# A hybrid two-block layer on Trainium2: a ninth weight tile, the last two pairs' down products last, and three pieces of work moved

## The chip, the cores and the metric

One core of a Trainium2 chip runs the whole program. The metric is the device time of one execution in microseconds (us), median of several. TensorE multiplies (PE in the rows; PEld its weight loads), VectorE (DVE), ScalarE (ACT) and GpSimd (POOL) do the rest, SyncE (SP) issues nearly all DMAs. Data are held in SBUF, 128 partitions; matrix products end in PSUM, eight banks of 128 x 512 float32.

## The reference

Two blocks work on 512 tokens of width 1024 in float32. The first is a mixer (state space and windowed attention) and a mixture of 64 experts, the second a mixer (neighbourhood attention, "na", and gated linear attention) and an MLP. What the change touches:

```python
# first block: 512 tokens, 8 groups of 8 experts, the two best of one group
expert_id = g_sel[:, None] * EXPERTS_PER_GROUP + top_local
gate = jax.nn.softmax(top_logit, axis=-1) * p_group
...
hid = jax.nn.silu(xb @ w_gate[e]) * (xb @ w_up[e])     # 1024 x 512 each
return hid @ w_down[e]                                 # 512 x 1024
...
y = jnp.zeros_like(t).at[tok_sorted].add(y_buf[dest] * flat_g[order][:, None])
# between the blocks
x = rmsnorm(h, norm_final)
# second block
n = rmsnorm_2(h, ln_g)
proj = n @ w_in                                        # q, k, v of na, and the gated part
```

## The kernel before

A planner orders the instructions of each engine from the text of the kernel; `pin` keeps an instruction in program order on its engine, and `order(a, b)` puts b behind a.

**Weights.** Each expert has three matrices of 2 MiB, 384 MiB in all. They come through a ring of eight SBUF tiles of 16 KB a partition: three of `ringp`, two of `ring2`, the two that hold A1 and A2 in the first block (`w16x`), and one of `ring3`, which is opened in `moe` where the mixer's pools lay. `ring` (line 119) takes the next tile, `load` (149) cuts the load into pieces, and SyncE's queue issues them in the order gate, up, down of each pair. A piece is issued as soon as its part of the tile has been read. For the last pair `pair` (137) loads the two experts' tiles in turn, piece by piece.

**Pairs.** `experts` goes over 32 pairs of experts, 64 slots for each expert, so that a pair's 128 rows fill the partitions. For pair i: gate and up products of the rows `xg` into two banks `pj` (line 991; 32 records a product), silu and product to `hid`, four transposes, `hT`, then the down products in two halves (`y`, `tp`), each split into a rounded part and its rest (`yH`, `yL`). A 0/1 matrix `ST` (made by `way` from the tokens of the slots) brings the rows back to H: `combine` makes two products (yH, yL) for each of 4 token tiles and 2 halves and adds the bank to H (line 1157, and the sum at 1160). The sums of pair i - 1 are made in pair i by `bring`.

**Rows.** The tokens of the slots are found by `values` for two pairs at a time (`slots`, L828), fetched from DRAM by GpSimd's indirect DMA (`fetch`, L843) into four tiles `rows`, and turned by `gained` into `xg` (two buffers, L1018) one pair ahead. Slots that nobody has are left out of the fetch, so the rows are zeroed once before (line 984).

**Ahead of pair 0.** The router's last choices run on VectorE (`choose`, `gather_first`: `eq` at 939, `S` at 940). The rows of pair 0 are made by products with H (L943), then turned. `split_values` (815 to 817) prepares on GpSimd what `values` needs; the zeroing (984) and the counting tile `tt` (988) stand ahead of it in GpSimd's order.

**The last pair.** It does not wait for H to be complete. `Begin` (the start of the second block) turns H, with all pairs up to 30 in it, into eight PSUM banks (`turn`, line 1704, four transposes a bank), the last pair's rows are added to the banks by two products each (`mm(p, y, ST)`), and `split` rounds them to `n2H`, `n2L`. Then `combine` brings the last pair to H, and `norms` loads the second block's first weights `wv` (line 1720) and makes the factors `r`. Eight of pair 30's sums stand inside the last gate product:

```python
if last and p is pg and j in (2, 5):
    bring(4)
```

**The second block's start.** `neighbours` makes four value projections (L199, L178 to 180), sends `r` to DRAM and reads it back in another order as `rc` (lines 1362 and 1365), and only then turns the values into seven tiles `v` scaled by `rc` (1376 to 1381), ahead of the projections of q and k (`project`). `attend` comes one head pair later than `project`. Each product of three terms is made from a rounded part and its rest, split by ScalarE (158) and VectorE (159).

Of the kernel before, what the change touches and what calls it, by code (L numbers as in the profile page):

```python
# [28 lines left out]
class Net:  # L29
# [83 lines left out]
    def ring(self, shape, dma, parts=1):  # L113
# [698 lines left out]
    def split_values(self):  # L812
# [4 lines left out]
        Pl.tensor_tensor(self.parts10[:, :, :, 1], v, self.parts10[:, :, :, 0].bitcast(FT), OP.subtract)  # L817
# [145 lines left out]
    def experts(self, keep, pool, front, inner, then):  # L963
        nc, i = self.nc, self.ins
        mm = nc.tensor.matmul
# [6 lines left out]
        def weights(e0):  # L972
            n = 4 if e0 < 12 else 4 if e0 == 62 else 2
            if e0 == 62:
                return [self.pair(shape, (w[62], w[63])) for shape, w in (([P, KT, 512], wg), ([P, KT, 512], wu),
                                                                          ([P, 4, D], wd))]
            return ([self.ring([P, KT, 512], wg[e0 + s], 8 if e0 == 2 else n) for s in range(2)],
                    [self.ring([P, KT, 512], wu[e0 + s], n) for s in range(2)],
                    [self.ring([P, 4, D], wd[e0 + s], n) for s in range(2)])
        ahead = None  # L980
# [7 lines left out]
        nc.gpsimd.iota(tt, pattern=[[1, T]], base=-1023, channel_multiplier=0, allow_small_or_imprecise_dtypes=True)  # L988
# [51 lines left out]
        self.split_values()  # L1040
# [3 lines left out]
        def bring(n):  # L1044
            for _ in range(min(n, len(todo))):
                self.combine(*todo.pop(0), pin=True)

        for i in range(32):
# [3 lines left out]
            G, U, Dn = ahead or weights(e0)  # L1052
            ahead = None
            pg, pu = self.psum("pj"), self.psum("pj")
            X = Xs.pop(i)
            for W, p in ((G, pg), (U, pu)):
                for j in range(KT):
# [3 lines left out]
                    if last and p is pg and j in (2, 5):  # L1061
                        bring(4)
                if i == 0 and p is pg:
                    values(0)
            if i == 0:
                chosen(1)
            if last:
# [19 lines left out]
            hT = pool.tile([P, 4, P], FT, name="hT", bufs=1)  # L1087
# [9 lines left out]
            def down(y, s, j, hs):  # L1097
                mm(y[64 * s:64 * s + 64, :], hT[:, j, 64 * s:64 * s + 64], Dn[s][:, j, hs], start=j == 0, stop=j == 3)
            if not last:
                for half, hs in enumerate(halves):  # L1100
# [7 lines left out]
                    todo.extend((ST, yH, yL, t, hs) for t in range(NT))  # L1108
                if i == 0:
                    values(1)  # L1110
                    for _ in gained(1):
                        evicted()
            else:
                ys = [self.psum(t) for t in ("y", "pj")]
# [4 lines left out]
                if begin:  # L1119
                    turned += [begin.turn(k) for k in (4, 5)]  # L1120
                parts = []
                for y in ys:
                    yH = pool.tile([P, 512], FR, name="yH")
                    yL = pool.tile([P, 512], FR, name="yL")
                    self.split(yH, yL, y, g)
                    parts.append((yH, yL))
                if begin:
                    turned.append(begin.turn(6))
                    for k in range(KT):
                        p = turned[k]  # L1130
                        for x, y in enumerate(parts[k // 4]):
                            mm(p, y[:, k % 4 * P:k % 4 * P + P], ST, start=False, stop=x == 1)
                        begin.split(k, p)
                        if k == 0:
                            turned.append(begin.turn(7))
# [17 lines left out]
    def combine(self, ST, yH, yL, t, hs, n=P, pin=False):  # L1153
        nc, h = self.nc, self.H
        p = self.psum("sc")
        for k, y in enumerate((yH, yL)):
            m = nc.tensor.matmul(p, ST[:n, t * P:(t + 1) * P], y[:n], start=k == 0, stop=k == 1)  # L1157
# [16 lines left out]
    def overflow(self, keep, pool, front):  # L1174
# [5 lines left out]
        orow = front.tile([64, D], FT, name="orow", tag="xg", bufs=2)  # L1180
        nc.gpsimd.memset(orow, 0.0)
# [3 lines left out]
        with tc.If(self.count > 0):  # L1185
            with tc.For_i(0, self.count, 1):
# [50 lines left out]
                for half in range(2):  # L1237
# [7 lines left out]
                    for t in range(NT):  # L1245
                        self.combine(ST, yH, yL, t, hs, 64)
# [95 lines left out]
    def neighbours(self, small, pool, wp, mixp, w_in, A):  # L1342
# [29 lines left out]
        v = []  # L1372
        for n in range(7):
            p = self.psum("tp")
            for j in range(4):
# [419 lines left out]
```

## Time and profile before

| | |
|---|---|
| three runs | 2061.43, 2054.8 and 2062.07 us |
| the profiled execution | 2057.0 us, span 2055.2 us |
| mean granted TensorE clock | 0.982 of full speed |
| TensorE busy | 1943.0 us, 95% |
| VectorE, ScalarE, GpSimd busy | 955.6, 533.8 and 196.3 us |
| bytes moved by DMA | 494.25 MB |

The first block's mixer takes the first 380 us or so, the router and the start of the experts lie around 380 to 440, the experts go on to about 1372, and the second block follows. Times in rows count from the first instruction of the span. A timeline row has start, length, engine, line, operation, out<-in, form and count; a row with a count merges neighbours of one kind, and its length runs to the end of the last. A granted clock of 1.00 is 2.4 GHz and 0.50 is 1.2 GHz.

### The profile page before, as it was taken

How to read it: one execution, taken by the hardware profiler on the slowest of the kernel's cores; microseconds unless marked ns; L12 is line 12 of the kernel's file. 1: busy time of each engine (PE TensorE's matmuls, PEld its weight loads, DVE VectorE, ACT ScalarE, POOL GpSimd, SP SyncE). 2: the span in 40 equal slices, each digit the busy share in tenths (PEclk: the TensorE clock that was granted, in tenths of full speed). 3: DMA queues.
4: the chain of work that ended last, by engine and by line, in shares of the span. 5: the costliest groups of instructions: out<-in, count | busy, mean ns of one | idle time of the engine just before them, and what ended most of it. 6: DMA issues, size and time to landing. Idle time of an engine off the chain costs nothing.

```text
span 2055.2 us, 24059 instructions
## 1 busy us (share of the span) xinstructions
PE 1943.0 (95%) x9519; PEld 1228.8 (60%) x9519; DVE 955.6 (46%) x1896; ACT 533.8 (26%) x899; POOL 196.3 (10%) x248
## 2 busy tenths in 40 slices
PE   7999999989999999989999999998999999999998
PEld 6788777734444444434434434446777778888886
DVE  5764667733543234244324323334564764343345
ACT  5773535311100000000000000024342433232232
POOL 5211324110000000000000000003201110000000
PEclk9999999999999999999999999999999999999999
DMA  7312122779999999999999999973212112213211
GB/s 201 113 42 82 46 78 82 287 299 416 415 423 425 424 424 424 424 424 424 425 425 424 421 421 425 423 252 67 90 42 82 42 42 92 94 71 123 90 74 41
DMA packets 114778, 494.25 MB, mean 240 GB/s; under 512 B 16492, under 2 KB 23091, under 8 KB 74984
## 3 DMA queue, kind: packets, MB, share of 16 engines
q1 hardware_dynamic: 107720, 483.63, 58.8%
q0 software_dynamic: 6352, 6.96, 1.5%
q10 hardware_dynamic: 592, 2.10, 0.3%
q8 instruction: 76, 1.25, 0.2%
q14 instruction: 38, 0.31, 0.0%
HBM read 500.68 MB, written 6.15 MB: 247 GB/s over the span
## 4 chain that ended last, share of the span: by engine, by line
PE 46%; DMA 44%; DVE 5%; ACT 3%; issue 1%; POOL 0%; SPq 0%; DVEq 0%; ACTq 0%; POOLq 0%
DMA w<-in_w_down 14%; DMA w<-in_w_up 14%; DMA w<-in_w_gate 13%; PE pj L179 7%; PE pj L178 7%; PE pj L180 7%; PE sc L179 3%; PE sc L178 3%; PE sc L180 3%; PE pj L991 2%; DMA w<-in_w_in 1%; DVE M L697 1%; PE y L180 1%; PE y L178 1%; PE y L179 1%
## 5 line engine op out<-in xcount | busy, mean ns | idle before, releaser
L991 PE MATMUL pj<-w,xg 128*64 128x512 f32 x1536 | 369.1, 612 | 39.4 <-DMA w<-in_w_up 36.4
L991 PEld LDWEIGHTS pj<-w,xg 128*64 128x64 f32 x1536 | 126.8, 141 | 270.8 <-issue 202.1
L159 DVE TENSOR_TENSOR wL<-w,wH 128x1024 fp32r<-128x1024 f32 x135 | 167.3, 1240 | 202.3 <-ACT wH L158 201.7
L1079 DVE SCALAR_TENSOR_TENSOR hid<-pj,slots,hid 128x512 f32<-128x512 f32 x32 | 24.1, 752 | 458.2 <-PE pj L991 458.2
L158 ACT CAST wH<-w 128x1024 fp32r<-128x1024 f32 x136 | 142.3, 1047 | 339.8 <-PE pj L179 165.9
L1160 DVE TENSOR_TENSOR H<-sc,H 128x512 f32<-128x512 f32 x256 | 161.5, 683 | 10.8 <-PE sc L1157 8.3
L991 PE MATMUL pj<-w16x,xg 128*64 128x512 f32 x512 | 125.1, 602 | 10.5 <-DMA w16x<-in_w_up 10.5
L1157 PE MATMUL sc<-yH,ST 128*128 128x512 f32 x256 | 113.2, 442 | 0.6 <-DVE H L1160 0.6
L1088 ACT COPY hT<-tp 128x512 f32<-128x512 f32 x32 | 18.8, 586 | 346.4 <-PE tp L1086 346.4
L843 POOL DMA_INDIRECT rows<-hd,tok x31 | 31.1, 1002 | 802.8 <-issue 642.0
L180 PE MATMUL pj<-n3H,wL 128*128 128x512 f32 (+1 forms) x272 | 103.6, 381 | 0.8 <-DVE wL L159 0.8
L178 PE MATMUL pj<-n3H,wH 128*128 128x512 f32 (+1 forms) x272 | 103.6, 381 | 0.0
L179 PE MATMUL pj<-n3L,wH 128*128 128x512 f32 (+1 forms) x272 | 103.5, 380 | 0.0
L178 PE MATMUL pj<-A,wH 128*128 128x512 f32 x240 | 97.8, 407 | 4.0 <-ACT wH L158 2.8
L1157 PE MATMUL sc<-yL,ST 128*128 128x512 f32 x256 | 101.2, 395 | 0.0
L179 PE MATMUL sc<-wL,mixH 128*128 128x512 f32 x252 | 98.5, 391 | 0.0
L178 PE MATMUL sc<-wH,mixH 128*128 128x512 f32 x252 | 98.4, 391 | 0.0
L180 PE MATMUL sc<-wH,mixL 128*128 128x512 f32 x252 | 98.2, 390 | 0.0
L179 PE MATMUL pj<-A,wH 128*128 128x512 f32 x240 | 97.6, 407 | 0.0
L180 PE MATMUL pj<-A,wL 128*128 128x512 f32 x240 | 96.8, 403 | 0.5 <-DVE wL L159 0.5
L991 PEld LDWEIGHTS pj<-w16x,xg 128*64 128x64 f32 x512 | 47.8, 138 | 82.2 <-issue 60.1
L991 PE MATMUL y<-w,hT 128*64 128x512 f32 x384 | 91.8, 599 | 0.7 <-ACT hT L1088 0.7
(571 smaller groups left out, 3322.2 us busy)
## 6 DMA issues: line engine op xcount, KB each, us to landing
w<-in_w_down SPq DMA_DIRECT2D x78, 1024.0 KB, 19.5
w<-in_w_up SPq DMA_DIRECT2D x76, 1024.0 KB, 20.7
w<-in_w_gate SPq DMA_DIRECT2D x76, 1024.0 KB, 19.6
w<-in_w_ff SPq DMA_DIRECT2D x16, 2048.0 KB, 8.7
w16x<-in_w_gate SPq DMA_DIRECT2D x28, 1024.0 KB, 19.8
w16x<-in_w_up SPq DMA_DIRECT2D x28, 1024.0 KB, 21.1
w<-in_w_in SPq DMA_DIRECT2D x12, 2048.0 KB, 11.2
w16x<-in_w_down SPq DMA_DIRECT2D x24, 1024.0 KB, 19.8
```

The costliest lines, as they stand in the source:

```text
L158: a = nc.scalar.copy(H, src)
L159: b = (engine or nc.vector).tensor_tensor(L, src, H.bitcast(FT), OP.subtract)
L178: m = mm(out, lH, rH, start=first, stop=False)
L179: mm(out, lH, rL, start=False, stop=False)
L180: mm(out, lL, rH, start=False, stop=last)
L697: nc.vector.tensor_tensor(t, t, cb[g], OP.mult)
L843: self.nc.gpsimd.indirect_dma_start(out=rows, out_offset=None, in_=self.hd[:, :], in_offset=bass.IndirectOffsetOnAxis(ap=tok, axis=0), bou ...
L991: return self.pin(nc.tensor.matmul(*a, **k))
L1079: V.scalar_tensor_tensor(hid, pu, r, hid, op0=OP.mult, op1=OP.mult)
L1088: nc.scalar.copy(hT.rearrange("p j s -> p (j s)"), p)
L1157: m = nc.tensor.matmul(p, ST[:n, t * P:(t + 1) * P], y[:n], start=k == 0, stop=k == 1)
L1160: nc.vector.tensor_tensor(h[:, t, hs], p, h[:, t, hs], OP.add)
```

## The change

- The ring has nine tiles: `ring3` has two. For their room `rows` has two tiles in place of four, `xg` one in place of two, `ST` two in place of three.
- Two of GpSimd's three memsets go (the overflow's own as well, which no run here enters); the third and the counting tile come behind `split_values`.
- With two tiles, `gained(1)` comes ahead of `values(1)` in pair 0.
- The loads of the last two pairs come in the order gate and up of 60 and 61, gate and up of 62 and 63, then the downs of 60 and 61, then those of 62 and 63.
- Pair 30's downs are made behind pair 31's gate and up products. Both pairs' rows are added into the turned banks, and `combine` adds both pairs' four parts in one bank for each sum into H. The turns of H, now with the pairs up to 29 in it, are pinned, three behind the last up product, three behind the downs of pair 30, two behind those of pair 31.
- `wv` goes into the ring tile that held expert 62's up matrix, in place of a new `ringp` tile.
- The turned values are made behind the second projection in place of ahead of the first.

```diff
-            p = self.rings[0 if self.held is None else (0, 0, 1, 1, 0, 0, 0, 2)[k]]
+            p = self.rings[0 if self.held is None else (0, 0, 1, 1, 0, 0, 0, 2, 2)[k]]
...
-            self.rings = [self.ringp, self.ring2, ctx.enter_context(tc.tile_pool(name="ring3", bufs=1, reuse_waits="tile"))]
+            self.rings = [self.ringp, self.ring2, ctx.enter_context(tc.tile_pool(name="ring3", bufs=2, reuse_waits="tile"))]
...
-        ST = pool.tile([P, T], FR, name="ST", bufs=3)
+        ST = pool.tile([P, T], FR, name="ST", bufs=2)
...
-            n = 4 if e0 < 12 else 4 if e0 == 62 else 2
-            if e0 == 62:
-                return [self.pair(shape, (w[62], w[63])) for shape, w in (([P, KT, 512], wg), ([P, KT, 512], wu),
-                                                                          ([P, 4, D], wd))]
...
+            if e0 == 60:
+
+                late.extend((lambda: one(dn, wd, 60), lambda: self.pair(dn, (wd[62], wd[63]))))
+                return [(one(up, wg, 60), one(up, wu, 60), None),
+                        (self.pair(up, (wg[62], wg[63])), self.pair(up, (wu[62], wu[63])), None)]
...
-        self.rows = [front.tile([P, D], FT, name=f"rows{n}", bufs=1) for n in range(4)]
-        for r in self.rows[1:]:
-            nc.gpsimd.memset(r, 0.0)
-
-
-        tt = self.tt = front.tile([P, T], FT, name="tt", bufs=1)
...
+        self.rows = [front.tile([P, D], FT, name=f"rows{n}", bufs=1) for n in range(2)]
...
-                    self.fetch(self.rows[2 * (q % 2) + x], tok[:, x:x + 1])
+                    self.fetch(self.rows[x], tok[:, x:x + 1])
...
-            x = front.tile([P, KT, P], FT, name="xg", bufs=2)
-            r = self.rows[pair % 4]
+            x = front.tile([P, KT, P], FT, name="xg", bufs=1)
+            r = self.rows[pair % 2]
...
-        self.split_values()
+        last = self.split_values()
+
+        zero = nc.gpsimd.memset(self.rows[1], 0.0)
+
+        tt = self.tt = front.tile([P, T], FT, name="tt", bufs=1)
...
+        for x in (zero, count):
+            self.order(last, x)
...
-                    if last and p is pg and j in (2, 5):
-                        bring(4)
...
+            if i == 30:
+                downs30, downs31 = [d() for d in late]
...
-            turned = [begin.turn(k) for k in range(4)] if last and begin else []
+                lastp = inner.enter_context(tc.tile_pool(name="lasty", bufs=2, reuse_waits="tile"))
+
+            turned = [begin.turn(k) for k in range(3)] if last and begin else []
...
+                downs, ST0 = before
+                pairs = [(ST0, downs())]
+
+                def added(k, p, pairs, stop):
+                    ys = [(S, y) for S, parts in pairs for y in parts[k // 4]]
+                    for n, (S, y) in enumerate(ys):
+                        mm(p, y[:, k % 4 * P:k % 4 * P + P], S, start=False, stop=stop and n == len(ys) - 1)
+                if begin:
+                    for k in range(6):
+                        if k > 2:
+                            turned.append(begin.turn(k))
+                        added(k, turned[k], pairs, False)
+                ys = [self.psum("pj") for _ in range(2)]
...
                     for k in range(KT):
...
+                        if k > 5:
+                            turned.append(begin.turn(k))
+                        added(k, turned[k], pairs[k < 6:], True)
+                        begin.split(k, turned[k])
                 for t in range(NT):
-                    for (yH, yL), hs in zip(parts, halves):
-                        self.combine(ST, yH, yL, t, hs)
+                    for half, hs in enumerate(halves):
+                        self.combine([(S, *y[half]) for S, y in pairs], t, hs)
...
-    TAGS = ("sc", "sc", "sc", "tp", "tp", "pj", "y", "sc")
+    TAGS = ("sc", "sc", "sc", "y", "tp", "tp", "sc", "sc")
...
-        t = net.ringp.tile([P, 4096], FT, name="w16", tag="w16")
+
+        t = net.held[6] if net.held else net.ringp.tile([P, 4096], FT, name="w16", tag="w16")
...
         ahead = project(0)
         for j in range(4):
             now, ahead = ahead, project(j + 1) if j < 3 else None
+            if j == 0:
+
+                v = []
+                for n in range(7):
...
+                mix = self.mixtile(mixp)
```

## Rows read from the trace of the kernel before

**Rows 1.** The page, part 2: GB/s moved in 40 equal slices.

```profile
GB/s 201 113 42 82 46 78 82 287 299 416 415 423 425 424 424 424 424 424 424 425 425 424 421 421 425 423 252 67 90 42 82 42 42 92 94 71 123 90 74 41
```

**Rows 2.** Windows: length, busy by engine, granted clock, DMA share, GB/s.

```profile
500.00:1240.00 740.00, 696.24 (x3172) 308.50 (x3170) 269.61 (x556) 65.51 (x99) 24.77 (x25) 0.98 1.01 423
...
1440.00:2055.00 615.00, 592.53 (x2966) 478.30 (x2964) 310.25 (x519) 201.13 (x311) 33.99 (x52) 0.98 0.21 74
```

**Rows 3.** TensorE's waits, 420 to 1320: total us, times, longest.

```profile
PE pj L991 <- DMA w<-in_w_up: 36.4, 17, 3.8
PE pj L991 <- DMA w16x<-in_w_up: 10.5, 6, 2.8
```

**Rows 4.** Windows ahead of pair 0, columns as in rows 2.

```profile
412.00:416.00 4.00, 2.70 (x5) 1.28 (x5) 2.60 (x14) 0.42 (x2) 0.66 (x2) 0.50 0.00 0
...
420.00:422.00 2.00, 2.00 (x12) 0.72 (x10) 0.67 (x5) 1.11 (x2) 0.43 (x2) 1.00 0.00 0
```

**Rows 5.** Timeline of SyncE's queue: start, length, engine, line, DMA, count.

```profile
401.40 4.35 SPq L149 DMA_DIRECT2D w<-in_w_gate  x8
421.48 6.90 SPq L149 DMA_DIRECT2D w<-in_w_up  x8
...
1417.06 4.47 SPq L1365 DMA_DIRECT2D rc<-r2d  x7
```

**Rows 6.** Timeline of TensorE; in brackets idle time before, and releaser.

```profile
406.67 1.96 PE L943 MATMUL tp<-H,S 128*128 128x512 f32 x4
...
412.45 0.21 PE L901 MATMUL sc<-M,before 128*128 128x64 bf16 x1 [3.73 <-DVE first L894]
...
413.56 3.78 PE L943 MATMUL tp<-H,S 128*128 128x512 f32 x4 [0.85 <-DVE S L940]
...
419.51 7.09 PE L991 MATMUL pj<-w,xg 128*64 128x512 f32 x32 [0.34 <-DVE xg L1020]
...
1295.02 0.60 PE L1018 MATMUL pj<-ident,rows 128*128 128x128 f32 x4
```

**Rows 7.** Line 137, the last pair's loads in 1300 to 1400.

```profile
L137 SPq DMA_DIRECT2D w<-in_w_down x6: 327/328/328, 1331.3 to 1343.7; - x6
...
DMA to landing us min/median/max: 14.7/19.7/19.8
```

**Rows 8.** Timeline of TensorE from pair 30's up product on.

```profile
1316.58 7.08 PE L991 MATMUL pj<-w,xg 128*64 128x512 f32 x30 [2.38 <-DMA w<-in_w_up]
...
1329.01 3.65 PE L991 MATMUL y<-w,hT 128*64 128x512 f32 x16
...
1372.48 0.66 PE L1704 MATMUL y<-ident,H 128*128 128x128 f32 x4 [0.71 <-DVE yL L172]
```

**Rows 9.** Window behind the last down, columns as in rows 2.

```profile
1376.50:1405.00 28.50, 28.50 (x124) 22.79 (x122) 21.39 (x32) 16.27 (x26) 6.07 (x10) 1.00 0.27 98
```

**Rows 10.** Timeline of TensorE at the attention values.

```profile
1419.96 1.97 PE L1376 MATMUL tp<-ident,vT 128*128 128x128 f32 x8 [7.83 <-DVE v L1381]
```

**Rows 11.** The chain that ended last, at the second block's start.

```profile
1405.42 11.56 DMA r2d<-r
```

**Rows 12.** Timeline of VectorE, ahead of pair 0 and at the values.

```profile
405.46 0.35 DVE L939 TENSOR_SCALAR eq<-it,keys 128x256 f32<-128x256 f32 x1
...
409.22 3.02 DVE L939 TENSOR_SCALAR eq<-it,keys 128x256 f32<-128x256 f32 x1
...
1419.15 0.75 DVE L1381 TENSOR_SCALAR v<-tp,rc 128x512 f32<-128x512 f32 x1 [11.82 <-DMA rc<-r2d]
```

**Rows 13.** Timeline of GpSimd: the zeroing, and a late fetch.

```profile
409.37 2.73 POOL L984 MEMSET rows<- 128x1024 f32 x3
...
1274.32 0.99 POOL L843 DMA_INDIRECT rows<-hd,tok  x1 [0.30 <-issue]
```

**Rows 14.** Line 843, all fetches of rows: us to landing.

```profile
DMA to landing us min/median/max: 6.6/8.7/10.9
```

**Rows 15.** Window behind the wait for the values, columns as in rows 2.

```profile
1420.00:1445.00 25.00, 25.00 (x112) 20.25 (x113) 12.26 (x12) 7.02 (x8) 8.08 (x9) 0.91 0.12 32
```

More of the change, by code (lines that the diff above doesn't have):

```diff
@@ L1051, in experts @@
             last = i == 31
-            G, U, Dn = ahead or weights(e0)
-            ahead = None
+            ahead = ahead or weights(e0)
+            G, U, Dn = ahead.pop(0)
             pg, pu = self.psum("pj"), self.psum("pj")
@@ L1066, in experts @@
                 chosen(1)
+            if i == 30:
+                downs30, downs31 = [d() for d in late]
+            if i > 29:
+                Dn = downs31 if last else downs30
             if last:
@@ L1086, in experts @@
                 self.pin(nc.tensor.transpose(p[:, j * P:(j + 1) * P], hid[:, j::4], self.ident))
-            hT = pool.tile([P, 4, P], FT, name="hT", bufs=1)
+            hT = (lastp if last else pool).tile([P, 4, P], FT, name="hT", bufs=1)
             nc.scalar.copy(hT.rearrange("p j s -> p (j s)"), p)
@@ L1095, in experts, with down, downs @@
                 values(q + 1)
-            def down(y, s, j, hs):
+            def down(y, s, j, hs, hT=hT, Dn=Dn):
                 mm(y[64 * s:64 * s + 64, :], hT[:, j, 64 * s:64 * s + 64], Dn[s][:, j, hs], start=j == 0, stop=j == 3)
-            if not last:
+            def downs(down=down, g=g):
+                parts = []
                 for half, hs in enumerate(halves):
@@ L1107, in experts @@
                     self.split(yH, yL, y, g)
-                    todo.extend((ST, yH, yL, t, hs) for t in range(NT))
+                    parts.append((yH, yL))
+                return parts
+            if i < 30:
+                todo.extend((ST, *y, t, hs) for y, hs in zip(downs(), halves) for t in range(NT))
                 if i == 0:
-                    values(1)
                     for _ in gained(1):
                         evicted()
-            else:
-                ys = [self.psum(t) for t in ("y", "pj")]
+                    values(1)
+            elif not last:
+                before = downs, ST
+            else:
+                downs, ST0 = before
[10 more added lines that the diff above has]
+                ys = [self.psum("pj") for _ in range(2)]
                 for j in range(4):
@@ L1118, in experts @@
                             down(y, s, j, hs)
-                if begin:
-                    turned += [begin.turn(k) for k in (4, 5)]
                 parts = []
-                for y in ys:
-                    yH = pool.tile([P, 512], FR, name="yH")
-                    yL = pool.tile([P, 512], FR, name="yL")
+                for half, y in enumerate(ys):
+                    yH = lastp.tile([P, 512], FR, name="yH")
+                    yL = pool.tile([P, 512], FR, name="yl", tag="hid", bufs=2) if half else lastp.tile([P, 512], FR, name="yL", bufs=1)
                     self.split(yH, yL, y, g)
                     parts.append((yH, yL))
+                pairs.append((ST, parts))
                 if begin:
-                    turned.append(begin.turn(6))
                     for k in range(KT):
[L1130 to L1135, printed above, removed]
+                        if k > 5:
+                            turned.append(begin.turn(k))
+                        added(k, turned[k], pairs[k < 6:], True)
+                        begin.split(k, turned[k])
                 for t in range(NT):
-                    for (yH, yL), hs in zip(parts, halves):
-                        self.combine(ST, yH, yL, t, hs)
+                    for half, hs in enumerate(halves):
+                        self.combine([(S, *y[half]) for S, y in pairs], t, hs)
                 if begin:
@@ L1179, in overflow @@
         at = keep.tile([P, 1], FT, name="at")
-        orow = front.tile([64, D], FT, name="orow", tag="xg", bufs=2)
-        nc.gpsimd.memset(orow, 0.0)
+        orow = self.rows[0][:64]
         nc.gpsimd.memset(at, 0.0)
@@ L1371, in neighbours @@
         G = [bias(h) for h in range(2)]
[L1372 to L1375, printed above, removed]
-                nc.tensor.transpose(p[:, j * P:(j + 1) * P], vT[:, j, 64 * n:64 * n + P], self.ident)
-            t = pool.tile([P, T], FT, name=f"v{n}", bufs=1)
-            if n & 1:
-                nc.scalar.activation(t, p, AF.Copy, scale=rc[:, n:n + 1])
-            else:
-                V.tensor_scalar(t, p, rc[:, n:n + 1], None, op0=OP.mult)
-            v.append(t)
-        mix = self.mixtile(mixp)
         wq = self.ring([P, KT, 512], w_in[:, :, 0:512])
@@ L1452, in neighbours @@
             now, ahead = ahead, project(j + 1) if j < 3 else None
+            if j == 0:
+                v = []
+                for n in range(7):
+                    p = self.psum("tp")
+                    for x in range(4):
+                        nc.tensor.transpose(p[:, x * P:(x + 1) * P], vT[:, x, 64 * n:64 * n + P], self.ident)
+                    t = pool.tile([P, T], FT, name=f"v{n}", bufs=1)
+                    if n & 1:
+                        nc.scalar.activation(t, p, AF.Copy, scale=rc[:, n:n + 1])
+                    else:
+                        V.tensor_scalar(t, p, rc[:, n:n + 1], None, op0=OP.mult)
+                    v.append(t)
+                mix = self.mixtile(mixp)
             if j == 3:
```

37 lines of the change are left out of this document (22 added, 15 removed).

## The prediction, made before the result

> **What bounds the kernel now.** First the page's strip of bytes [rows 1]: a plateau of 415 to 425 GB/s through the middle of the span, with far less on both sides, so the kernel has two regimes. The plateau as one window [rows 2]: DMA share 1.01 at 423 GB/s, TensorE busy 696 of 740 us. TensorE's own waits there [rows 3]: 23 on up weights, together 46.9 us, and little else. So the weight stream sets the pace of the experts, and TensorE has 46.9 / 30 = 1.6 us to spare in each pair. A byte that lands earlier at the head of the stream moves everything up to its end; an instruction saved inside the stage moves nothing.
>
> Then the two edges of the stream. Ahead of it the engines are idle [rows 4]: no byte in 412 to 416 and none in 420 to 422. What they wait for is in SyncE's queue [rows 5]: the eight pieces of the ring's eighth tile are issued from 401.4 to 405.8, the next tile only from 421.48, 2 us after TensorE begins pair 0 at 419.51 [rows 6], because all eight tiles are full until then. Behind it: the last piece of the last pair is issued at 1343.7, and pieces of that line take 14.7 us at the least [rows 7], so the stream ends near 1358.4. TensorE does not wait for that: its last wait on a weight ends at 1316.58 [rows 8], and up to the end of the last down, 0.71 us before 1372.48, its own order binds it. From 1376.5 to 1405 it is busy without a gap [rows 9], then it stands 7.83 us for the first attention values [rows 10], behind a round trip through DRAM of 11.56 us [rows 11]. From 1440 on it is busy 592 of 615 us [rows 2], so what is won by then reaches the end.
>
> **The change, step by step.**
>
> *Zeroing moved.* The selection's comparison takes 0.35 us at 405.46 and 3.02 us at 409.22 [rows 12]; three memsets of GpSimd run from 409.37 to 412.10 [rows 13]. The path to pair 0 goes through it: TensorE idles 3.73 us and then works on its result [rows 6]. Two memsets go and the third moves behind the values' split, when TensorE already has pair 0: 3.02 - 0.35 = 2.7 us earlier. After that idle time the granted clock is 0.50, the lower of its two levels [rows 4], and the four last gathering products take 3.78 us against 1.96 before it [rows 6]. If the shorter gap leaves the clock up, 1.8 us more are saved: bounds 2.7 and 4.5. What is left of the gap (about 408.7 to 410.9, with tiny products in it) could go either way, so I take 3.5 us, near the middle.
> The Trainium skill ("SBUF: State Buffer", Who interferes with whom) says that GpSimd and a VectorE instruction in a two-port mode exclude each other for one whole instruction. By that the comparison would wait for one of the memsets, 0.9 us; here it waited for all three, 2.7 us, and the row decides.
> The Trainium skill ("TensorE: Matmul & The Clock Gate", Part 1) says that the clock has two levels and follows how busy the engine has lately been. The rows agree on the levels; by it the larger bound holds if the gap left is short enough, which no run here shows yet.
>
> *Ninth tile.* A tile of 2.097 MB takes 4.95 us at 423 GB/s [rows 2]. The idle engines can take it before pair 0 starts if its memory is free: what lay there belongs to the mixer, as with the eighth tile, which was let go at 401.4 [rows 5]. Issued behind that at 405.8, it lands by about 416, when pair 0 begins. The stream then restarts one tile ahead: 4.95 us, bounds 0 (memory not free) and 4.95. Rate and bytes stay, and TensorE's 46.9 us of waits absorb the shift. Together the stream runs S = 3.5 + 4.95 = 8.5 us earlier, bounds 2.7 and 9.5.
>
> *Half the row buffers, one turned buffer xg, two ST.* Cost taken: nothing. A fetch issued at 1274.32 [rows 13] lands within 10.9 us [rows 14] and is turned at 1295.02 [rows 6]: 9.8 us of cover. Its buffer's former rows are turned earlier in the same pair, ahead of the products that find the tokens; xg is written after the up product that reads it, on TensorE's own order; ST of two pairs back is no longer read. If the cover went, TensorE would wait at the turning. The number of fetches stays, so the stream carries no more.
>
> *Both downs last.* In the times of before, S still to come off. The up product of pair 30 starts at 1316.58; sums, turns and hidden rows go on to 1329.0 as now [rows 8]. Then gate and up of pair 31 without the eight sums and 16 turning transposes that break them now: 2 x 7.1 us [rows 6], to 1343.2. Their weights are there: the four downs behind them, 8.4 MB, need the last 19.8 us of the stream, so they land by 1338.6, and the second half of the up product is reached at 1339.7. Three turns of 0.66 us [rows 8] and the four transposes of hid, as long: 1345.9. The down of 30 has as many records, 7.1 us, but its last piece lands 9.9 us (4.19 MB) ahead of the stream's end, at 1348.5; it ends near 1353.8. Twelve products into the turned rows at 0.23 us (28.5 us for 124 [rows 9]), 2.8 us, and three turns, 2.0 us: 1358.6. By then the last down has landed: 7.1 us, 1365.7. Before: 1371.8. Against these 6.1 us stand four products of pair 30 for the last two turned tiles, 0.9 us, and its 16 combining products, 3.7 us, which before were done by then; in sum 16 products more are made. I take off 0.5 us for more exchanges between forms. 1.0 us is left as gain. Bounds: 4.6 us lost, if downs that land late eat the whole 6.1 us but for the exchanges; 6 us gained, if VectorE's sums and not the products set the pace after the last down.
> The loads of w_in go into expert 62's up tile, read up to 1343.2; SyncE comes to them after 1343.7 [rows 7], so they wait for nothing new, and the loads behind them are wanted only from 1405 on.
>
> *Values moved.* Seven tiles of attention values wait for rc. With two heads' projections ahead of them TensorE has 4 x 24 products of 0.23 us, 22 us, after r is known; the trip takes 13.7 us from 1405.42 [rows 11] to the first value at 1419.15 [rows 12] and the seven reads are issued over 4.47 us [rows 5], 18.2 us: covered. Gone are the 7.83 us and the low clock behind them: 0.91 over 25 us [rows 15], 2.3 us. Against it, 28 transposes stand together and each bank waits for a copy of 0.75 us [rows 12]: 0 to 2 us, taken 1. Net 9 us, bounds 0 and 10.1 us.
>
> **Sum.** 8.5 + 1.0 + 9.0 = 18.5 us off the profiled execution's 2057.0 us (its span is 2055.2): 2038.5. The median of the three runs shown, 2061.4, is 4.4 us above that execution, by which it would be 2043; I take 2041.
>
> **The rivals.**
> *The wait of the values only changes its place* (chance 0.15). VectorE and ScalarE work in order; if a value's copy stands ahead of the splits for the next projection, VectorE stands for rc as it does now, 11.82 us [rows 12], and TensorE runs dry behind it. For it: that is how the queue stands now. Against: the values come behind 96 products in the new text. Gain 9.5 us: 2050.
> *The ninth tile does nothing* (0.10): its memory is held until pair 0 by something later than the mixer. For it: all of the front lies further up. Against: the eighth tile came at 401.4. Gain 18.5 - 4.95 = 13.5 us: 2046.
> *The end is longer* (0.08): the pinned turns wait in order for downs and splits, and the 16 more products are paid in full, 4.6 us lost in place of 1.0 gained. Gain 12.9 us: 2047.
> *Rows fetched too late* (0.05), the one on the other side. With two row tiles a fetch may not start before the former rows are turned. Were it late by more than the 9.8 us of cover and the 3.2 us that TensorE can spare in two pairs, each further us would be paid in all 15 rounds. At 15 us late that is 2 x 15 = 30 us lost: 2071. It decides from 14.2 us on (1.2 x 15 = 18). Against it: the turn stands just ahead of the fetch.
> *As forecast:* 0.60. The last 0.02 are for slower without a reason that I see.
>
> **How the numbers follow.** The forecast's own range is 2035 to 2049: 4.5 at the clock, 10.1 at the values and 5 at the end give 24.6 us; 2.7, 5 and a loss of 2 give 10.7 us. The whole range goes from all upper bounds off the profiled execution (9.5 + 6 + 10.1 = 25.6 us: 2031) to the values' rival with the lower clock bound and a loss of 1 at the end (2053). About 0.5%, 10.3 us, is what a measurement here can tell from no change. Faster by more: nearly all of the forecast, most of the second and third rival, half of the first, 0.79. Within: 0.15. Slower: 0.06.
>
> **What would show it.** The comparison at 0.35 us and pair 0 beginning near 416; bytes flowing between 412 and 417; the up product of pair 30 starting near 1308; gate and up of pair 31 in one run of 14 us; the last down ending near 1357; no wait of TensorE between r and the first scores, and a granted clock of 1.00 there. I am wrong if the stream's end does not move by 8 us, if TensorE waits for rows inside the pairs, or if the 7.8 us turn up at another line.

## The result, and the profile after

The changed kernel takes 2036.8 us (median of 4 runs, 2031.6 to 2038.6) against 2061.8 for the kernel before: a ratio of 0.988, 95% interval 0.985 to 0.9911. Run again later the ratio was 0.9881 (0.9864 to 0.9899). The prediction said 2041, 2031 to 2053. The profiled execution takes 2035.3 us, its span is 2033.5; before, 2057.0 and 2055.2. In the spans 21.7 us are gone; the profiled execution before lies 4.7 us below its median, so the spans show less than the medians.

The page's strip of bytes after, to be laid beside [rows 1]:

```profile
GB/s 203 115 43 83 27 70 111 259 342 415 415 424 426 424 424 424 424 424 425 424 424 424 422 422 424 422 320 68 91 42 83 43 52 83 118 50 123 99 68 42
```

The plateau has the rate that it had. Windows of 2 us ahead of pair 0, columns as in [rows 2]; they answer to [rows 4]:

```profile
412.00:414.00 2.00, 1.85 (x4) 0.68 (x4) 1.81 (x10) 0.20 (x1) 0.00 (x0) 0.85 0.97 385
414.00:416.00 2.00, 1.27 (x4) 0.53 (x4) 0.51 (x5) 1.15 (x2) 0.00 (x0) 0.50 1.04 416
...
418.00:420.00 2.00, 2.00 (x8) 0.47 (x5) 0.79 (x5) 0.56 (x2) 0.82 (x3) 0.50 0.00 0
420.00:422.00 2.00, 2.00 (x12) 0.79 (x10) 0.00 (x0) 0.00 (x0) 1.02 (x2) 0.95 0.17 16
```

Where no byte moved in 412 to 416, 385 and 416 GB/s do now. The granted clock is low in both kernels; here it falls between 412 and 414 and is 0.50 from there to 420. SyncE's queue tells which bytes these are (against [rows 5]):

```profile
402.66 4.40 SPq L149 DMA_DIRECT2D w<-in_w_gate  x8
407.10 13.95 SPq L149 DMA_DIRECT2D w<-in_w_up  x5
```

Behind the eighth tile's pieces the first up pieces of the ninth follow at once, at 407.1. TensorE (against [rows 6] and [rows 8]; in brackets the idle time before):

```profile
407.93 1.96 PE L943 MATMUL tp<-H,S 128*128 128x512 f32 x4
...
411.05 0.19 PE L901 MATMUL sc<-M,before 128*128 128x64 bf16 x1 [1.07 <-DVE first L894]
...
412.15 2.60 PE L943 MATMUL tp<-H,S 128*128 128x512 f32 x4 [0.88 <-DVE S L940]
...
417.38 8.47 PE L986 MATMUL pj<-w,xg 128*64 128x512 f32 x32
...
1303.46 14.16 PE L986 MATMUL pj<-w,xg 128*64 128x512 f32 x64
...
1322.98 7.09 PE L986 MATMUL pj<-w16x,xg 128*64 128x512 f32 x32
1329.89 7.04 PE L986 MATMUL pj<-w,xg 128*64 128x512 f32 x32
...
1352.07 7.09 PE L986 MATMUL pj<-w,hT 128*64 128x512 f32 x32
...
1359.90 0.51 PE L986 MATMUL sc<-ST,yL 128*128 128x512 f32 x1 [0.29 <-DVE yL L172]
```

The wait for the router's last choice is 1.07 us for 3.73, but the products behind it run in the low clock, and pair 0's gate product too: 8.47 us for 7.09. At 1303.46 gate and up of pair 30 are one run of 64 records, so its up product starts at about 1303.46 + 14.16 / 2 = 1310.5, 6.0 us earlier. Gate and up of pair 31 follow one another at 1322.98 and 1329.89, and the last down, at 1352.07, ends at 1359.2. VectorE's timeline, against [rows 12]:

```profile
410.49 0.35 DVE L939 TENSOR_SCALAR eq<-it,keys 128x256 f32<-128x256 f32 x1
...
1388.07 0.17 DVE L1769 COPY r<-rr 128x8 f32<-128x8 f32 x1
...
1419.71 0.71 DVE L1481 TENSOR_SCALAR v<-tp,rc 128x512 f32<-128x512 f32 x1
```

The comparison takes 0.35 us for 3.02. The factors r are known at 1388.07, 17 us earlier than before (1405.23), and the first value's copy has no wait for rc. GpSimd's timeline, against [rows 13]:

```profile
419.38 0.23 POOL L817 TENSOR_TENSOR parts<-vals,parts 128x20 fp32r<-128x20 f32 x1
419.55 0.96 POOL L1037 MEMSET rows<- 128x1024 f32 x1
```

The one memset stands at 419.55, behind the values' split. Inside the stage TensorE's waits are nearly those of [rows 3]:

```profile
PE pj L986 <- DMA w<-in_w_up: 45.2, 22, 3.7
...
PE pj L986 <- DMA w16x<-in_w_gate: 1.1, 1, 1.1
```

No row names a wait for fetched rows in a pair. At the second block's start, where before 7.83 us were lost [rows 10]:

```profile
1395.26 1.05 PE L187 MATMUL sc<-ident,r 128*128 128x128 f32 x8
...
1418.56 1.03 PE L1476 MATMUL tp<-ident,vT 128*128 128x128 f32 x8
...
1420.47 1.09 PE L1476 MATMUL tp<-ident,vT 128*128 128x128 f32 x8 [0.25 <-DVE v L1481]
```

From the token row (L187) TensorE goes on to the values without a gap and waits 0.25 and then 0.18 us there. The windows behind it (against [rows 15]) have the clock at 1.00 for 0.91:

```profile
1395.00:1420.00 25.00, 25.00 (x118) 20.17 (x116) 10.04 (x10) 6.75 (x7) 9.74 (x12) 1.00 0.71 45
1420.00:1445.00 25.00, 24.34 (x148) 17.59 (x144) 16.76 (x45) 10.76 (x25) 4.53 (x6) 1.00 0.30 101
```

In the kernel before the token row starts here:

```profile
1405.45 1.16 PE L187 MATMUL sc<-ident,r 128*128 128x128 f32 x8 [0.32 <-DVE r L1737]
```

The three stretches add up: 6.0 us to pair 30's up product; from there to the token row 84.7 us for 88.9, 4.2 us; from the token row to the end of the span 638.2 us for 649.8, 11.5 us. Together 21.7.

### The profile page after: what moved, and what is told of

Same layout as the page of the kernel before. It is cut to its first block, busy times and chain, and to the rows that moved or that the text cites. A ratio compares the mean times of both kernels' runs of the same rounds, so it can differ in the third digit from the quotient of the medians.

```text
span 2033.5 us, 24005 instructions
## 1 busy us (share of the span) xinstructions
PE 1936.5 (95%) x9535; PEld 1217.1 (60%) x9535; DVE 948.4 (47%) x1891; ACT 534.1 (26%) x899; POOL 192.1 (9%) x245
## 5 line engine op out<-in xcount | busy, mean ns | idle before, releaser
L986 PE MATMUL pj<-w,xg 128*64 128x512 f32 x1696 | 470.1, 608 | 45.9 <-DMA w<-in_w_up 45.2
L986 PEld LDWEIGHTS pj<-w,xg 128*64 128x64 f32 x1696 | 154.8, 140 | 332.2 <-issue 255.0
L1190 DVE TENSOR_TENSOR H<-sc,H 128x512 f32<-128x512 f32 x248 | 156.6, 683 | 6.2 <-PE sc L1187 3.5
L986 PE MATMUL pj<-w16x,xg 128*64 128x512 f32 x352 | 151.7, 614 | 1.1 <-DMA w16x<-in_w_gate 1.1
L986 PE MATMUL y<-w,hT 128*64 128x512 f32 x336 | 78.0, 599 | 0.6 <-DMA w<-in_w_down 0.6
L986 PE MATMUL tp<-w,hT 128*64 128x512 f32 x336 | 76.5, 592 | 0.0
```

The lines of the kernel that those rows point to most:

```text
L986: return self.pin(nc.tensor.matmul(*a, **k))
L1190: nc.vector.tensor_tensor(h[:, t, hs], p, h[:, t, hs], OP.add)
```

## The experiments

First theory: the terms of the prediction (stream, end, values) are separate and add. Rivals: the end and the values overlap, since the new end makes r early by itself; the ninth tile does nothing; the halved buffers cost something. Times below are ratios to the kernel before on the same chip, from medians of 4 to 12 executions; 0.001 is 2.06 us, the intervals are about +-0.0015, and single executions of one kernel differ by several us. Traces are therefore also compared from one fixed instant, the start of the gathering products of the third token tile (L943; 406.67 before, 407.93 after), the last thing that is alike in all of them. That does not take out all of the noise: up to pair 30's up product the kernel before and two other traces with the same front (the values alone, the new end alone) take 909.9, 913.4 and 912.2 us.

**The values alone, and all but the values.**

```diff
-        v = []
-        for n in range(7):
...
         for j in range(4):
             now, ahead = ahead, project(j + 1) if j < 3 else None
+            if j == 0:
+                v = []
+                for n in range(7):
```

> The kernel before with one edit: the seven value tiles are turned and scaled, and the mix tile taken, after the second group of projections instead of ahead of the first. First theory (the terms of the prediction add): the wait of 7.83 us for the values goes, and with it the low clock behind it, 9 us in all, bounds 0 and 10.1: about 2052.7 us, a ratio of 0.9956. Second theory (the terms interact: the new order of the last pair makes the factors early as well) says the same of this run, 9 to 10 us, and differs on the next one. Rival (the wait only changes place): TensorE waits as long a little later, and the ratio is 1.000, within 1 us.

> The changed kernel with the values turned where they stood before. First theory: what the move is worth does not depend on the rest, so the time rises by 9 to 11.5 us, to 2046 to 2048, a ratio to before of 0.9925 to 0.9935. Second theory: with the last pairs' downs last, the factors are known 7 us ahead of the token row and no longer with it; TensorE would reach the values 6.7 us after the token row, about 1402, and the reordered factors are read at about 1402.7 and land 2 to 3 us later, so the wait is 3 to 5 us: 2040 to 2042, a ratio of 0.989 to 0.990.

The first gave 0.9958 (0.9942 to 0.9973), 8.7 us. The second gave 0.9928 (0.991 to 0.9946), 9.7 us more than the changed kernel's 0.9881. The rival of the overlap expected 0.989 to 0.990 there. The move of the values is worth the same with either end, as far as the intervals tell: the overlap is refuted. The timeline of TensorE in the run of the values alone,

```profile
1412.30 1.16 PE L187 MATMUL sc<-ident,r 128*128 128x128 f32 x8 [0.32 <-DVE r L1739]
...
1419.76 0.50 PE L180 MATMUL pj<-n2H,wL 128*128 128x512 f32 x1 [0.23 <-DVE wL L159]
```

has no wait for v, so the wait did not change its place. In the other run,

```profile
1394.16 1.05 PE L187 MATMUL sc<-ident,r 128*128 128x128 f32 x8
...
1405.27 1.11 PE L1405 MATMUL tp<-ident,vT 128*128 128x128 f32 x4 [7.28 <-ACT v L1408]
```

TensorE stands 7.28 us for the values: it runs dry at 1398.0, 3.8 us after the token row starts and not 6.7 as I had assumed, and the chain of waits

```profile
1387.22 14.54 DMA r2d<-r
...
1402.50 1.95 DMA rc<-r2d
```

shows the trip to DRAM longer, 14.54 us for the 11.56 of [rows 11]. It is so in every trace: from the issue of r's write to the first read behind it 11.4 to 11.8 us with the old end (six traces), 14.2 to 16.1 us with the new one (eight). With the new end the 2 MB load of `w_out` is issued 0.5 to 1.1 us ahead of r on SyncE's queue, with the old one 10.1 us ahead; that this is the cause was not tested.

**The zeroing alone.** Four row tiles stay.

```diff
-        for r in self.rows[1:]:
-            nc.gpsimd.memset(r, 0.0)
...
+        behind = self.split_values()
+        zero = [nc.gpsimd.memset(r, 0.0) for r in self.rows[1:]]
...
+        for x in zero + [count]:
+            self.order(behind, x)
```

> The kernel before with the zeroing of three row tiles and the counting tile placed behind the work that prepares the values on GpSimd; everything else stays. First theory: the comparison takes 0.35 us for 3.02, the fall of the clock ahead of pair 0 goes with it, 3.5 us in all (2.7 to 4.5), and the stream of weights carries it to the end: 2058.3 us, ratio 0.9983. Rival on the clock: the changed kernel shows the fall 2 us later, over the turned rows and the first gate product, so only some 2 us are left: 2059.7, ratio 0.999. Rival on the stream: what pair 0 gains is waited off on the next weights, and the ratio is 1.000. The profile tells them apart by the start of pair 0's gate product (before 419.51), its length (7.09) and the start of pair 30's up product (1316.58).

0.9983 (0.9971 to 0.9996), 3.5 us. TensorE's timeline:

```profile
407.17 1.96 PE L943 MATMUL tp<-H,S 128*128 128x512 f32 x4
...
411.38 3.68 PE L943 MATMUL tp<-H,S 128*128 128x512 f32 x4 [0.88 <-DVE S L940]
...
417.23 7.09 PE L985 MATMUL pj<-w,xg 128*64 128x512 f32 x32 [0.34 <-DVE xg L1014]
```

From the fixed instant to the end of pair 0's gate product it is 17.15 us, before 19.93: 2.8 us, the prediction's lower bound, with the low clock still there over the last gathering products (3.68 us). Counted from the fixed instant, 1.6 us are left at pair 30's up product and none at the token row, since in this trace, and not in that of the kernel before, the clock fell again at the last down; the 3.5 us rest on the times.

**The halved buffers, and the ninth tile on top.**

```diff
-        self.rows = [front.tile([P, D], FT, name=f"rows{n}", bufs=1) for n in range(4)]
+        self.rows = [front.tile([P, D], FT, name=f"rows{n}", bufs=1) for n in range(2)]
...
-            x = front.tile([P, KT, P], FT, name="xg", bufs=2)
+            x = front.tile([P, KT, P], FT, name="xg", bufs=1)
...
-            self.rings = [self.ringp, self.ring2, ctx.enter_context(tc.tile_pool(name="ring3", bufs=1, reuse_waits="tile"))]
+            self.rings = [self.ringp, self.ring2, ctx.enter_context(tc.tile_pool(name="ring3", bufs=2, reuse_waits="tile"))]
```

The first run has the row tiles, `xg` and `ST` halved; the last two lines are the second run's alone.

> The kernel before with two row tiles, one xg and two ST for four, two and three, and pair 1's rows turned ahead of the next fetch; eight weight tiles, the old zeroing, end and values. Prediction: nothing, 2060, ratio 1.000 within 0.001, since every row is fetched long before it is turned; as only one tile is zeroed, the comparison ahead of pair 0 waits less, which may give back 1 us. Rival (rows fetched too late): waits for rows in every second pair, 2 us slower or more.

> The run with the halved buffers, with a ninth weight tile in the room that they leave. Prediction's term for the ninth tile: 4.95 us less than that run, 2055, ratio 0.9975. What the traces show so far: from the gathering of the rows to pair 30's up product the eight-tile version of the changed kernel takes 909.0 us, the changed kernel 902.6 and 904.4, so 5.5 us: 2054.5. Rival (the ninth tile does nothing): the same time as the run with halved buffers.

Halved buffers: 0.998 (0.9968 to 0.9991), 4.1 us faster; the one memset that is left runs at 400.24 in that trace, ahead of the comparison, which takes 0.35 us, so this is the term of the zeroing by another road and no cost of the buffers shows. With the ninth tile: 0.9967 (0.9954 to 0.998), 2.7 us more, although here the memset (the second row, of GpSimd) stands beside the comparison:

```profile
411.04 1.24 DVE L939 TENSOR_SCALAR eq<-it,keys 128x256 f32<-128x256 f32 x1
```

```profile
411.18 0.94 POOL L984 MEMSET rows<- 128x1024 f32 x1
```

**The changed kernel with eight tiles.**

```diff
-            if self.held is not None and k in (4, 5):
+            if self.held is not None and k in (2, 3):
...
-            self.rings = [self.ringp, self.ring2, ctx.enter_context(tc.tile_pool(name="ring3", bufs=2, reuse_waits="tile"))]
+            self.rings = [self.ringp, self.ring2, ctx.enter_context(tc.tile_pool(name="ring3", bufs=1, reuse_waits="tile"))]
```

> The changed kernel with a ring of eight weight tiles, the rest as changed (the tiles of A1 and A2 are those that the last pair's up weights use, and the second block's first weights take the tile of the last pair's first gate weights). Prediction's term: the ninth tile is worth 4.95 us of earlier stream, bounds 0 and 4.95: 2041.7, ratio 0.9903. Rival (the ninth tile does nothing): 2036.8, ratio 0.988, and the up product of pair 30 starts as in the changed kernel, near 1310.5. By the first, it starts near 1315.5.

0.9898 (0.9878 to 0.9918), 3.5 us slower than the changed kernel. The times leave room from nothing to 9 us. The traces are clearer: pair 30's up product and the token row of this run,

```profile
1316.97 8.78 PE L986 MATMUL pj<-w,xg 128*64 128x512 f32 x30 [2.37 <-DMA w<-in_w_up]
...
1401.72 1.05 PE L187 MATMUL sc<-ident,r 128*128 128x128 f32 x8
```

come 909.0 and 993.75 us after the fixed instant, the changed kernel's 904.4 and 989.1 (902.6 and 987.3 in its first profile). The ninth tile is worth 4.6 to 6.4 us there, and 4.7 to the token row between the two runs of the pair above (998.73 and 994.01). Counted from the end of pair 0's gate product, which leaves out the clock ahead of it, all traces can be laid together: from there to pair 30's up product the six with eight tiles take 890.0 to 891.6 us, the eight with nine tiles 884.7 to 886.4, on average 5.4 us less. What comes ahead of that instant took 15.5 to 21.8 us, so a loss or gain at the head reaches pair 30 nearly whole.

**The old end, and the new end alone.**

```diff
-            elif not last:
-                before = downs, ST
-            else:
-                downs, ST0 = before
-                pairs = [(ST0, downs())]
...
+            else:
+                ys = [self.psum(t) for t in ("y", "pj")]
```

> The changed kernel again, unaltered, on the chip of the next three runs, so that they can be set against it as well as against the kernel before: a ratio of 0.988, some 2036 us.

> The changed kernel with the end of the expert stage as it was before: the downs of pair 30 before the gate of pair 31, its sums within that gate, the old order of loads; nine tiles, the two row tiles, the late zeroing and the moved values stay. Prediction's term: both downs last are worth 1.0 us, so 2 us slower at most than the changed kernel run beside it, about +1.0. What the two traces show: from the last up weights to the token row the changed kernel is 4.1 us shorter, so +4 us. Rival (the new end is longer, for its two waits and what stands behind the last down): 3 us faster than the changed kernel.

> The kernel before with both downs last and their sums in the turned rows, and the loads in the order that this needs; eight tiles, four row tiles, the old zeroing and the values where they were. Prediction's term: 1.0 us faster, 2059, ratio 0.9995. What the traces show: the old end takes 88.9 to 90.6 us from pair 30's up product to the token row, the new one 84.5 to 84.8, so 4 to 6 us faster: 2055, ratio 0.9975. Rival (the gain of the end is taken back by the wait for the reordered factors, since the values stand where they stood): as the run without the move of the values showed 7.28 us of wait against 7.83 before, no.

The changed kernel again: 0.9881. With the old end: 0.9914 (0.9899 to 0.9929), 6.8 us slower. The new end alone on the kernel before: 0.9974 (0.9962 to 0.9985), 5.4 us faster. So it is worth 5 to 7 us by the times. Up product of pair 30 and token row, the changed kernel first, then the one with the old end:

```profile
1310.61 7.08 PE L986 MATMUL pj<-w,xg 128*64 128x512 f32 x30 [2.18 <-DMA w<-in_w_up]
...
1395.32 1.05 PE L187 MATMUL sc<-ident,r 128*128 128x128 f32 x8
```

```profile
1308.98 8.78 PE L985 MATMUL pj<-w,xg 128*64 128x512 f32 x30 [2.21 <-DMA w<-in_w_up]
...
1399.55 1.16 PE L187 MATMUL sc<-ident,r 128*128 128x128 f32 x8 [0.32 <-DVE r L1737]
```

84.7 us against 90.6. Pair 30's up product takes 8.78 us in the second for 7.08, in the low clock, and with the old end that is paid: 88.9 us in the kernel before, where it takes 7.08 us, 90.6 to 90.7 in the four traces where it takes 8.78. The new end takes 84.7 to 84.8 us either way, since the downs of pair 30 then wait for their weights, as in the changed kernel here, or, where the up product was slow, do not:

```profile
1340.12 1.94 PE L986 MATMUL y<-w,hT 128*64 128x512 f32 x8 [0.16 <-DMA w<-in_w_down]
1342.54 1.50 PE L986 MATMUL y<-w,hT 128*64 128x512 f32 x5 [0.49 <-DMA w<-in_w_down]
```

So the new end is worth 4.2 us where that product has the full clock and 5.9 where it has not. In the old end TensorE still stands for ScalarE and VectorE behind the last down; the timeline of the kernel before shows it:

```profile
1374.38 0.51 PE L199 MATMUL pj<-n2H,wH 128*128 128x512 f32 x1 [0.78 <-ACT n2H L171]
1375.41 0.66 PE L1704 MATMUL sc<-ident,H 128*128 128x128 f32 x4 [0.52 <-DVE n2L L172]
```

with the 0.71 us of [rows 8] these are 2.0 us. The changed kernel has one such wait, 0.29 us. The parts of the new end (order of loads, pinned turns, place of `wv`, sums) were not run apart.

**The clock ahead of pair 0, and the downs of pair 30 in turn.** The first run adds thirteen products that nobody reads, the second adds the order of the loads to it, the third has nine products and the loads in turn.

```diff
+        if c > 1:
+            p = self.psum("pj")
+            for _ in range(9 if c == 2 else 4):
+                x = self.pin(nc.tensor.matmul(p, self.ones16, self.it.bitcast(BF)[:, :512]))
...
-                late.extend((lambda: one(dn, wd, 60), lambda: self.pair(dn, (wd[62], wd[63]))))
+                late.extend(lambda e=e: self.pair(dn, (wd[e], wd[e + 1])) for e in (60, 62))
```

> The changed kernel with thirteen bfloat16 products that nobody reads (128 x 512, into a bank that is free) in the gaps ahead of pair 0: five before the wait for the router's last choice, four before the last product of the row gathering, four before the first turns. First theory (the gaps of 1.07 and 0.88 us bring the low clock, and it costs the last gathering 1.6 us, the turns 0.8 us and the first gate product 1.4 us): the clock stays at 1.00 from 408 to 422, pair 0's gate product takes 7.0 us and ends 2 to 3 us earlier, of which the stream of weights carries most: 2 to 2.8 us faster than the changed kernel. Rival (the weights set the end of the expert stage): pair 0 ends earlier and the time is the same within 1 us. Rival (the products stand in the way): slower by up to 1 us.

> The run with the products that nobody reads, and the downs of pair 30 loaded piece by piece in turn from its two experts, as those of pair 31 are. In the changed kernel the downs of pair 30 wait 0.16 and 0.49 us for the second expert's weights. First theory: these waits go and the token row comes 0.65 us earlier. Rival: the last pieces land when they landed before, and nothing changes.

> The changed kernel with the downs of pair 30 loaded in turn from both experts, and nine bfloat16 products that nobody reads ahead of the last product of the row gathering, without the four ahead of the turns: there the copies of the rows waited for them (2.94 us on VectorE). First theory: the clock stays at 1.00 and the turns begin 0.7 us earlier than in the run with thirteen such products, which measured 2033.5: 2033, ratio 0.987. Rival: without the last four the clock falls over the turns and pair 0, and the time is that of the changed kernel less 0.65 us, 2035, ratio 0.988.

Products alone: 0.9883 (0.9867 to 0.9898); with the loads in turn 0.9872 (0.9853 to 0.9891); nine products and the loads in turn 0.9867 (0.9851 to 0.9883), 2032.7 us. The clock did stay at 1.00 in all three. The gain of 2 to 2.8 us that was expected of the first is not there in its time. The gathering and pair 0 of the last one,

```profile
408.14 1.96 PE L943 MATMUL tp<-H,S 128*128 128x512 f32 x4
...
416.57 7.09 PE L994 MATMUL pj<-w,xg 128*64 128x512 f32 x32 [0.33 <-DVE xg L1023]
```

take 15.52 us from the fixed instant to the end of the gate product; in the changed kernel it is 17.92 in both profiles. The waits of 0.16 and 0.49 us for the second down weights are gone in the last two, and the token row comes 84.5 and 84.0 us behind pair 30's up product for 84.7; in the first run they are gone too, by the slow up product. But the times are not told apart from the changed kernel's: 2.7 us at the most between medians, with intervals that overlap. The last version is the fastest measured and beats the kernel before by 1.3%; that it beats the changed one is not shown.

## Why the prediction came out, step by step

- **Zeroing, 3.5 us taken, 2.7 to 4.5.** Right by its time: 3.5 us by itself. Both bounds were met in traces, the lower where the clock fell (2.8 us in the zeroing alone), the upper where it did not: in the run without the move of the values the same front took 15.51 us, 4.4 less than before. In both profiles of the changed kernel the clock fell, later and for longer, and 2.0 us were left, less than the lower bound: the sum had the clock over the last gathering products, but not over pair 0's gate product (8.47 us for 7.09). In the run with nine tiles and the old zeroing only one memset, of 0.94 us, stood beside the comparison, which took 1.24 us, 0.89 more than alone; three in a row cost 2.7 us. The rule of the Trainium skill ("SBUF — State Buffer", Who interferes with whom), that GpSimd and a VectorE instruction in a two-port mode exclude each other for one whole instruction, agrees with the one memset and not with the three: VectorE did not get in between them.
- **Ninth tile, 4.95 us.** Right in size and mechanism: its loads start at 407.1 and flow from 412 to 416; 5.4 us over all traces, 2.7 and 3.5 by the times, whose intervals hold 4.95 too. That it does nothing is refuted by the traces, not by the times alone.
- **The stream, S = 8.5 us.** The run with the old end has front and values: 0.9914, of which the values make 0.0042. That leaves 0.0044, 9.1 us, with +-4.5. In the profile shown, the up product of pair 30 came 6.0 us earlier, 7.3 counted from the fixed instant and 5.5 in the changed kernel's second profile. The last piece of the last pair is issued at 1337.6, 6.1 us earlier, so the prediction's own sign, a stream's end that moves by 8 us, is not met between these profiles, and pair 0 began at 417.4 and not near 416. The clock of pair 0 makes the difference: it was full in the profile before and low in the changed kernel's. The two other traces with the front of before had it low as well, and against them (912.2 and 913.4 us) the changed kernel's 902.6 and 904.4 are 7.8 to 10.7 us.
- **Halved buffers, nothing.** Right: no waits for rows, and no loss in the run of their own. The rival of late rows is out.
- **Both downs last, 1.0 us taken.** This is the term that was mis-sized. The first part was right for the kernel as profiled: from the up product of pair 30 to the end of the last down 48.6 us, predicted 49.1, before 55.2. What I then took off for the work behind the last down, 0.9 + 3.7 + 0.5 us, was too much: from the last down's end to the token row it is 36.1 us for 33.7, 2.4 and not 5.1. The added products are there, but they run where TensorE before waited 2.0 us for splits, which my sum had left out. That gives 4.2 us between the two profiles and 5.4 to 6.8 in the timed runs. Up to 1.8 us of the difference is a term that the sum had at nothing: a low clock over pair 30's up product or the last down, which the old end pays and the new one takes up in its wait for weights. Five of six traces with the old end have it (90.5 to 90.7 us to the token row); only the kernel before, from which the sum was made, has not (88.9). Whether more is left the intervals do not tell. The rival that the end is longer is out.
- **Values moved, 9 us.** Right by the times: 8.7 us alone, 9.7 taken out of the changed kernel. Between the two profiles it is 11.5 us behind the token row, above the upper bound of 10.1; the waits at the copies came to 0.4 us where 1 was taken, and where the rest comes from stays open.
- **Sum.** Predicted 18.5 us, measured 24.5 (0.0119). The parts alone make 3.5 (zeroing) + 2.7 (ninth tile) + 5.4 (end) + 8.7 (values) = 20.3, and taken out of the changed kernel the last three are 3.5, 6.8 and 9.7: those alone with about +-3 us, those taken out with up to +-5, so the terms add as far as this can be measured. Of the 6 us by which the sum fell short, 4.4 to 5.8 are the end's. On top of it I had gone from 2038.5 to 2041 because the profiled execution lay below the median; the changed kernel's lies 1.5 us below its own. That 2038.5 would have lain nearer to the 2036.8 measured is luck: too small a gain off too low a start.

## What to carry over

A stage that is bound by its stream of bytes is paid at its two ends: what lands earlier at its head moves the whole stage, while the slack inside it swallows what is won or lost there. When work is moved behind a wait, count the idle time it will run in before charging it in full. And one profile carries noise as large as a small term: compare from an instant that all versions share, cut the span where the noise enters, and time the parts alone and taken out.

## What the runs showed of the hardware

The clock's fall ahead of pair 0 is not settled by the instructions: with the same front, and the same gaps of 1.07 and 0.88 us in it, the windows of 412 to 414 of the changed kernel's second profile and of the version without the move of the values are

```profile
412.00:414.00 2.00, 1.27 (x3) 0.24 (x2) 0.83 (x5) 0.86 (x2) 0.00 (x0) 0.50 1.04 418
```

```profile
412.00:414.00 2.00, 1.30 (x3) 0.68 (x4) 1.77 (x11) 0.28 (x2) 0.00 (x0) 1.00 0.97 353
```

0.50 against 1.00. The second runs 2.2 us later there; its clock is 1.00 in every window from 408 to 422. With nine or thirteen small products in the gaps it stayed at 1.00 in three executions of three, without them in one of three, the second window's (it fell in both profiles of the changed kernel): that the products keep it up is likely and not shown.

A low clock cost nothing where a wait for weights followed. In the run with thirteen products pair 30's up product takes 8.78 us,

```profile
1310.26 8.78 PE L994 MATMUL pj<-w,xg 128*64 128x512 f32 x30 [2.19 <-DMA w<-in_w_up]
...
1394.97 1.05 PE L187 MATMUL sc<-ident,r 128*128 128x128 f32 x8
```

for 7.08 in the changed kernel, and the token row still comes 84.7 us behind its start; the down product of pair 30, waits included, takes 7.3 us for 9.0. Where TensorE is the bound it does cost. With the old end the same 8.78 us for 7.08 put the token row 1.7 us off (90.6 us for 88.9). In the run of the values alone the mean granted clock of 1600 to 1700 was 0.91, before 0.95 and after 0.97, and it takes 642.7 us behind the token row, the seven other traces with moved values 638.2 to 639.7. Its span, 2055.0, shows nothing of the 8.7 us that its eight runs show: 7.1 us are gone behind the token row, but low clocks at pair 0 and pair 30 cost 3.4 and 1.7 us, and its front began 1.7 us later.
